# Cross entropy with label smoothing: first row in three tiles, second row in eleven of which nine follow into its buffers, first row's logarithm behind the second row's first exponential

## The chip, the cores and the metric

The kernel runs on one core of one Trainium2 chip. The metric is the device time in microseconds; times are medians. A *span* is the stretch from the first to the last traced instruction of one execution. It is shorter than the time.

## The reference

For each of 256 rows of 32000 float32 logits it computes the cross entropy against a smoothed one-hot target:

```python
log_probs = logits - max(logits); log_probs -= log(sum(exp(log_probs)))
target    = eps / C everywhere, plus (1 - eps) at the label
out       = -sum(target * log_probs)
```

Unfolded, a row's loss is `log(sum(exp(x))) - eps/C * sum(x) - (1 - eps) * x[label]`. The draw is from a normal distribution, and the kernel leaves the maximum out. Three things are needed of each row: the sum of exponentials, the sum of logits, and one gathered logit.

## The kernel before

Each of the 128 partitions holds two rows, streamed one after the other in tiles. For each tile ScalarE makes the exponentials (only their sum is kept, the elements go to a discard buffer) and VectorE the sum of logits. GpSimd gathers the labels' logits. At the end TensorE transposes the results into one row, for one contiguous output transfer; matmuls on a tile of row two warm its clock up for that.

```python
WIDTHS = ((8000, 8000, 8000, 8000),
          (8000, 6272, 4736, 3648, 2688, 2048, 1536, 1216, 1024, 832))
RING_MIN = 4736      # wider or equal: one of three ring buffers; narrower: its own buffer
TURN_MAX = 3648      # wider: single discard buffer; narrower or equal: one of three in turn
# ... cut ...
def sum_exps(xt, w, out):
    if w > TURN_MAX:
        ja = junk.tile([P, max(WIDTHS[0])], BF16, name="ja", tag="ja")   # bufs=1
    else:
        ja = turn.tile([P, TURN_MAX], BF16, name="jt", tag="jt")         # bufs=3
    nc.scalar.activation(out=ja[:, :w], in_=xt[:, :w], func=AF.Exp, accum_out=out)
# ... cut: the first row's loop, then its halves added up ...
nc.scalar.activation(out=lse[:], in_=sums[:, 1, :], func=AF.Ln)   # before row two
# ... cut: row two, where the last exponential's sum goes to PSUM ...
nc.scalar.activation(out=lse[:], in_=elast[:], func=AF.Ln, bias=done[2][:, 1:2])
```

The softmax here doesn't subtract the row's maximum and nothing guards it: scores larger than these inputs give would overflow.

## Time and profile before

| | before |
|---|---|
| time, 3 runs | 84.93 us (84.86 to 85.04) |
| span of the profiled run | 83.2 us |
| last tile's VectorE sum starts (my landing clock) | 79.13 us |
| last exponential | 79.24 to 80.12 us |
| last logarithm starts | 80.20 us |
| busy: DVE, ACT | 45%, 71% of the span |

The busy share of 71% for ScalarE is an average over a first row with idle stretches of some 2.5 us between tiles and a second row with almost none from its second tile on. So one reads the second row. These timeline lines of the kernel before (start, length, engine, line, operation, idle time and what ended it) show the two exponentials of row two that write to the single discard buffer after another that did, and the first that does not:

```profile
57.77 5.43 ACT L188 ACTIVATE ja<-xt 128x6272 bf16<-128x6272 f32 x1 [0.50 <-DMA xt<-in_logits_dram]
63.10 0.19 ACT L188 ACTIVATION_READ_ACCUMULATOR ja<-xt 128x1 f32 x1
63.41 4.15 ACT L188 ACTIVATE ja<-xt 128x4736 bf16<-128x4736 f32 x1
67.47 0.19 ACT L188 ACTIVATION_READ_ACCUMULATOR ja<-xt 128x1 f32 x1
67.72 3.24 ACT L188 ACTIVATE jt<-xl 128x3648 bf16<-128x3648 f32 x1
```

The 6272 exponential and its accumulator read are over at 63.10 + 0.19 = 63.29; the next starts at 63.41, together with VectorE's sum of the same tile (63.42). It waited for data. Whatever it also had to wait for on its own engine lay inside that wait.

### The profile page before, as it was taken

To read this page: it belongs to the slowest core of one execution; us is meant where nothing else is said; L and a number is where in the kernel's file an instruction comes from. 1 tells how busy PE (TensorE), PEld (TensorE's weight loads), DVE (VectorE), ACT (ScalarE), POOL (GpSimd) and SP (SyncE) were. 2 spreads that over 40 slices of the span, in tenths; PEclk is the share of its full clock that TensorE was granted. 3 is DMA by queue.
4 is the path that set the end of the run, shared out by engine and by line. 5 is a ranking of instruction groups with operands and counts; after the bars stand their busy time and mean duration, and the time that the engine had idled before them with its cause. 6 is when DMAs were issued, how large, how long until landed. Compare 5 with 4: busy or idle time off the path is not lost.

```text
span 83.2 us, 230 instructions
## 1 busy us (share of the span) xinstructions
PE 7.0 (8%) x23; PEld 5.0 (6%) x23; DVE 37.1 (45%) x35; ACT 58.8 (71%) x31; POOL 5.7 (7%) x19
## 2 busy tenths in 40 slices
PE   0000000000000000000000010000000000899020
PEld 0000000000000000000000000000000000787000
DVE  0000005950495009910397017922944736754860
ACT  5000005997499809994399908997999999999960
POOL 3201640031000000000000040000000000000000
PEclk9999999999999999999999999999999999999995
DMA  5999999997999899989998998998999999999600
GB/s 131 416 416 408 454 423 462 477 447 323 477 493 431 369 431 493 446 369 416 493 462 354 416 439 386 495 447 370 428 420 414 442 407 415 412 414 412 256 0 0
DMA packets 2258, 32.77 MB, mean 394 GB/s; under 512 B 337, under 2 KB 338, under 8 KB 850
## 3 DMA queue, kind: packets, MB, share of 16 engines
q1 hardware_dynamic: 2018, 30.72, 87.4%
q10 hardware_dynamic: 144, 2.05, 5.8%
q0 software_dynamic: 96, 0.00, 0.1%
HBM read 32.77 MB, written 0.00 MB: 394 GB/s over the span
## 4 chain that ended last, share of the span: by engine, by line
DMA 64%; ACT 32%; issue 1%; SPq 0%; PE 0%; DVE 0%; ACTq 0%
DMA xt<-in_logits_dram 40%; DMA xl<-in_logits_dram 23%; ACT ja L188 17%; ACT jt L188 15%; SPq L167 0%; PE lse_t L193 0%; DVE res L284 0%; ACT lse L279 0%; ACTq L188 0%
## 5 line engine op out<-in xcount | busy, mean ns | idle before, releaser
L188 ACT ACTIVATE ja<-xt 128x8000 bf16<-128x8000 f32 (+2 forms) x7 | 43.9, 6276 | 20.1 <-DMA xt<-in_logits_dram 20.0
L173 DVE SCALAR_TENSOR_TENSOR jd<-xt 128x4000 f32<-128x4000 f32 (+2 forms) x7 | 27.7, 3954 | 33.6 <-DMA xt<-in_logits_dram 33.6
L188 ACT ACTIVATE jt<-xl 128x3648 bf16<-128x3648 f32 (+6 forms) x7 | 12.2, 1748 | 0.1
L173 DVE SCALAR_TENSOR_TENSOR jd<-xl 128x1824 f32<-128x1824 f32 (+6 forms) x7 | 7.9, 1125 | 5.2 <-DMA xl<-in_logits_dram 5.0
L270 PE MATMUL warm<-xl,ident 128*128 128x256 f32 x20 | 6.1, 471 | 21.4 <-DMA xl<-in_logits_dram 21.4
L270 PEld LDWEIGHTS warm<-xl,ident 128*128 128x128 f32 x20 | 4.8, 246 | 22.5 <-DMA xl<-in_logits_dram 21.7
L193 PE MATMUL loss_t<-ident,loss 128*1 128x128 f32 x1 | 0.4, 372 | 49.2 <-POOL loss L224 49.2
L193 PEld LDWEIGHTS loss_t<-ident,loss 128*1 128x1 f32 x1 | 0.1, 79 | 49.2 <-POOL loss L224 49.2
L226 DVE COPY res<-loss_t 1x128 f32<-1x128 f32 x1 | 0.3, 278 | 4.5 <-PE loss_t L193 4.5
L211 POOL TENSOR_TENSOR half<-sums 128x4 f32<-128x4 f32 x1 | 0.2, 198 | 28.2 <-ACT ja L188 28.2
L125 POOL DMA_INDIRECT gat<-in_logits_dram,flat_idx x2 | 2.0, 1004 | 0.7 <-POOL ident masks.py:199 0.4
L92 ACT ACT_TABLE_LOAD x1 | 1.3, 1283 | 0.9 <-PEq L311 0.9
L188 ACT ACTIVATION_READ_ACCUMULATOR ja<-xt 128x1 f32 x7 | 1.3, 186 | 0.0
L188 ACT ACTIVATION_READ_ACCUMULATOR jt<-xl 128x1 f32 x7 | 1.3, 181 | 0.0
L146 POOL TENSOR_SCALAR weighted<-gat 128x1 f32<-128x1 f32 x1 | 0.8, 763 | 5.8 <-DMA gat<-in_logits_dram,flat_idx 5.8
L105 POOL DMA_DIRECT2D lab<-in_labels_dram x1 | 0.8, 766 | 1.0 <-POOLq L311 1.0
L216 ACT ACTIVATE lse<-half 128x1 f32<-128x1 f32 x1 | 0.2, 203 | 0.6 <-POOL half L211 0.6
L173 DVE DVE_READ_ACCUMULATOR jd<-xt 128x1 f32 x7 | 0.6, 82 | 0.0
L173 DVE DVE_READ_ACCUMULATOR jd<-xl 128x1 f32 x7 | 0.6, 82 | 0.0
L117 POOL TENSOR_TENSOR flat_idx<-rowoff,lab 128x2 int32<-128x2 int32 x1 | 0.2, 197 | 5.4 <-DMA lab<-in_labels_dram 5.4
L193 PE MATMUL lin_t<-ident,done 128*1 128x128 f32 x1 | 0.3, 270 | 3.0 <-DVE done L263 3.0
L282 DVE COPY lin_row<-lin_t 1x128 f32<-1x128 f32 x1 | 0.3, 278 | 0.4 <-PE lin_t L193 0.4
(20 smaller groups left out, 3.8 us busy)
## 6 DMA issues: line engine op xcount, KB each, us to landing
xt<-in_logits_dram SPq DMA_DIRECT2D x4, 4000.0 KB, 21.1
xt<-in_logits_dram SPq DMA_DIRECT2D x1, 3136.0 KB, 19.4
xt<-in_logits_dram SPq DMA_DIRECT2D x1, 2368.0 KB
xt<-in_logits_dram SPq DMA_DIRECT2D x1, 2000.0 KB, 11.5
xt<-in_logits_dram ACTq DMA_DIRECT2D x1, 2000.0 KB, 13.2
xl<-in_logits_dram SPq DMA_DIRECT2D x1, 1824.0 KB, 19.5
xl<-in_logits_dram SPq DMA_DIRECT2D x1, 1344.0 KB, 22.3
xl<-in_logits_dram SPq DMA_DIRECT2D x1, 1024.0 KB, 24.3
```

Of the source, the lines that this page charges most:

```text
L92: nc.scalar.add_instruction(mybir.InstLoadActFuncSet(name=nc.get_next_instruction_name(), act_func_set_id=tbl, ins=[], outs=[],))
L105: nc.gpsimd.dma_start(out=lab[:], in_=labels.bitcast(I32).rearrange("(p f) -> p f", p=P))
L117: nc.gpsimd.tensor_tensor(out=flat_idx[:], in0=rowoff[:], in1=lab[:].rearrange("p (r two) -> p r two", two=2)[:, :, 0:1], op=ALU.add,)
L125: nc.gpsimd.indirect_dma_start(out=gat[:, r : r + 1], out_offset=None, in_=logits[:], in_offset=bass.IndirectOffsetOnAxis(ap=flat_idx[:, r ...
L146: nc.gpsimd.tensor_scalar(out=weighted[r], in0=gat[:, r : r + 1], scalar1=label_weight, scalar2=None, op0=ALU.mult,)
L173: return nc.vector.scalar_tensor_tensor(out=jd[:, :h], in0=xt[:, :h], scalar=1.0, in1=xt[:, h:w], op0=ALU.mult, op1=ALU.add, accum_out=out,)
L188: nc.scalar.activation(out=ja[:, :w], in_=xt[:, :w], func=AF.Exp, accum_out=out)
L193: nc.tensor.transpose(out=row[:], in_=column, identity=ident[:])
L211: nc.gpsimd.tensor_tensor(out=half[:], in0=sums[:, :, :n], in1=sums[:, :, n:], op=ALU.add)
L226: nc.vector.tensor_copy(out=res[:, :, r : r + 1], in_=loss_t[:])
L270: nc.tensor.matmul(warm[:], lhsT=ident[:], rhs=xt[:, i * WARM_COLS : (i + 1) * WARM_COLS], start=True, stop=True,)
L282: nc.vector.tensor_copy(out=lin_row[:], in_=lin_t[:])
```

## The change

The intent: ask for all of row one without waiting for a buffer to come free, let row two follow into the same three buffers, end on a narrower tile (640 columns in place of 832), and keep the first row's logarithm from making ScalarE wait for GpSimd. The core of the diff, cut:

```diff
 WIDTHS = (
-    (8000, 8000, 8000, 8000),
-    (8000, 6272, 4736, 3648, 2688, 2048, 1536, 1216, 1024, 832),
+    (9600, 11200, 11200),
+    (8320, 6528, 4672, 3392, 2496, 1856, 1408, 1088, 896, 704, 640),
 )
-RING_MIN = 4736
-TURN_MAX = 3648
+FOLLOW = (1, 2, 6)      # how many tiles of row two go into each buffer of row one
+TURN_MAX = 2496
-WARM_LEFT, WARM_COLS = 5, 256
+WARM_LEFT, WARM_COLS = 6, 256
 ... (cut: the three wide buffers and their slices)
+        with tc.issue_after(exps.ins):
+            nc.scalar.activation(out=lse[:], in_=total[:, 1, :], func=AF.Ln)
 ... (cut: two additions in a row on GpSimd in place of a tree; the copy of row one's result, now behind row two's first sum)
+        if t == 0:
+            finish_first_row(part, exps)
```

More of the change, by code (lines that the diff above doesn't have):

```diff
@@ L78 @@
     c_big = 1.0 - eps
-    ring = ctx.enter_context(tc.tile_pool(name="ring", bufs=3))
+    wide = ctx.enter_context(tc.tile_pool(name="wide", bufs=1))
     tail = ctx.enter_context(tc.tile_pool(name="tail", bufs=1))
@@ L154, with load @@
     res = small.tile([1, P, R], FP32, name="res", tag="res")
-    def load(w: int, col: int, name: str):
-        if w >= RING_MIN:
-            xt = ring.tile([P, max(WIDTHS[0])], FP32, name="xt", tag="xt")
-        else:
-            xt = tail.tile([P, w], FP32, name=name, tag=name)
+    assert R == 2 and len(FOLLOW) == len(WIDTHS[0])
+    buffers = []
+    for r in range(R):
+        for b, w in enumerate(WIDTHS[0]):
+            widths = WIDTHS[0][b : b + 1]
+            if r == 1:
+                t = sum(FOLLOW[:b])
+                widths = WIDTHS[1][t : t + FOLLOW[b]]
+            buf = wide.tile([P, w], FP32, name=f"wide{b}_{r}", tag=f"wide{b}")
+            assert sum(widths) <= w
+            at = 0
+            for v in widths:
+                buffers.append(buf[:, at : at + v])
+                at += v
+    for t in range(sum(FOLLOW), len(WIDTHS[1])):
+        w = WIDTHS[1][t]
+        buffers.append(tail.tile([P, w], FP32, name=f"tail{t}", tag=f"tail{t}")[:])
+    def load(w: int, col: int):
+        xt = buffers.pop(0)
         if col == 0:
@@ L166, in load @@
         else:
-            nc.sync.dma_start(out=xt[:, :w], in_=x[:, col : col + w])
+            nc.sync.dma_start(out=xt, in_=x[:, col : col + w])
         return xt
@@ L181, in sum_logits, with sum_exps @@
         )
-    def sum_exps(xt, w: int, out: bass.AP) -> None:
+    def sum_exps(xt, w: int, out: bass.AP):
         if w > TURN_MAX:
@@ L187, in sum_exps @@
             ja = turn.tile([P, TURN_MAX], BF16, name="jt", tag="jt")
-        nc.scalar.activation(out=ja[:, :w], in_=xt[:, :w], func=AF.Exp, accum_out=out)
+        return nc.scalar.activation(
+            out=ja[:, :w], in_=xt[:, :w], func=AF.Exp, accum_out=out
+        )
     def row_of(column: bass.AP, name: str):
@@ L194, in row_of, with finish_first_row @@
         return row
+    assert R == 2
     col = 0
-    for r in range(R - 1):
-        n = len(WIDTHS[r])
-        sums = small.tile([P, 2, n], FP32, name=f"sums{r}", tag=f"sums{r}")
-        for t, w in enumerate(WIDTHS[r]):
-            xt = load(w, col, f"xl{r}_{t}")
-            col += w
-            sum_logits(xt, w, sums[:, 0, t : t + 1])
-            sum_exps(xt, w, sums[:, 1, t : t + 1])
-        while n > 1:
-            assert n % 2 == 0
-            n //= 2
-            half = small.tile([P, 2, n], FP32, name=f"half{r}_{n}", tag=f"half{r}_{n}")
+    n = len(WIDTHS[0])
+    sums = small.tile([P, 2, n], FP32, name="sums", tag="sums")
+    for t, w in enumerate(WIDTHS[0]):
+        xt = load(w, col)
+        col += w
+        sum_logits(xt, w, sums[:, 0, t : t + 1])
+        sum_exps(xt, w, sums[:, 1, t : t + 1])
+    def finish_first_row(part, exps) -> None:
+        total = sums[:, :, 0:1]
+        for t in range(1, n):
+            acc = small.tile([P, 2, 1], FP32, name=f"acc{t}", tag=f"acc{t}")
             nc.gpsimd.tensor_tensor(
-                out=half[:], in0=sums[:, :, :n], in1=sums[:, :, n:], op=ALU.add
+                out=acc[:], in0=total, in1=sums[:, :, t : t + 1], op=ALU.add
             )
-            sums = half
-        lse = small.tile([P, 1], FP32, name=f"lse{r}", tag=f"lse{r}")
-        nc.scalar.activation(out=lse[:], in_=sums[:, 1, :], func=AF.Ln)
-        lin = small.tile([P, 1], FP32, name=f"lin{r}", tag=f"lin{r}")
-        nc.gpsimd.tensor_tensor(out=lin[:], in0=sums[:, 0, :], in1=weighted[r], op=ALU.add)
-        scaled = small.tile([P, 1], FP32, name=f"scaled{r}", tag=f"scaled{r}")
+            total = acc[:]
+        lin = small.tile([P, 1], FP32, name="lin0", tag="lin0")
+        nc.gpsimd.tensor_tensor(
+            out=lin[:], in0=total[:, 0, :], in1=weighted[0], op=ALU.add
+        )
+        scaled = small.tile([P, 1], FP32, name="scaled0", tag="scaled0")
         nc.gpsimd.tensor_scalar(
@@ L222 @@
         )
-        loss = small.tile([P, 1], FP32, name=f"loss{r}", tag=f"loss{r}")
+        lse = small.tile([P, 1], FP32, name="lse0", tag="lse0")
+        with tc.issue_after(exps.ins):
+            nc.scalar.activation(out=lse[:], in_=total[:, 1, :], func=AF.Ln)
+        loss = small.tile([P, 1], FP32, name="loss0", tag="loss0")
         nc.gpsimd.tensor_tensor(out=loss[:], in0=scaled[:], in1=lse[:], op=ALU.add)
-        loss_t = row_of(loss[:], f"loss_t{r}")
-        nc.vector.tensor_copy(out=res[:, :, r : r + 1], in_=loss_t[:])
+        loss_t = row_of(loss[:], "loss_t0")
+        with tc.issue_after(part.ins):
+            nc.vector.tensor_copy(out=res[:, :, 0:1], in_=loss_t[:])
     r = R - 1
-    n = len(WIDTHS[r])
+    last = len(WIDTHS[r]) - 1
     elast = psum.tile([P, 1], FP32, name="elast", tag="elast")
@@ L240 @@
     for t, w in enumerate(WIDTHS[r]):
-        left = n - 1 - t
-        xt = load(w, col, f"xl{r}_{t}")
+        left = last - t
+        xt = load(w, col)
         col += w
@@ L247 @@
         if left == 0:
-            sum_exps(xt, w, elast[:])
+            exps = sum_exps(xt, w, elast[:])
         elif left <= 2:
-            sum_exps(xt, w, pairs[2 - left][:, 1:2])
+            exps = sum_exps(xt, w, pairs[2 - left][:, 1:2])
         else:
-            sum_exps(xt, w, esum[:, t : t + 1])
+            exps = sum_exps(xt, w, esum[:, t : t + 1])
+        if t == 0:
+            finish_first_row(part, exps)
         if left == 2:
```

## The prediction

> **What bounds the kernel now.** I read the chain that ended last first, then the slices of DMA activity, then the timeline of the second row tile by tile, and last the groups of instructions with the shapes kept apart.
>
> The chain and the DMA slices of the page of the kernel before:
>
> ```profile
> DMA  5999999997999899989998998998999999999600
> ...
> DMA 64%; ACT 32%; issue 1%; SPq 0%; PE 0%; DVE 0%; ACTq 0%
> ```
>
> Transfers are busy from the second slice to slice 38 of 40, so the stream of 32.77 MB hardly stops (a 7 or 8 is followed by fuller slices). The ACT share of the chain is not a second bound: the chain goes back through ScalarE in stretches in which a buffer's release by ScalarE started a later transfer, or in which ScalarE and the transfers kept step. Nor do the long waits of the DMA-issuing queue (24.7 us for VectorE, 10.4 us for ScalarE, 16.2 us for earlier transfers) cost stream time. The fourth wide tile is asked for when the first is read, at 20.35 us; the second has then not quite landed and the third is queued whole. Something was in the queue throughout.
>
> How fast is the stream? The VectorE sum of a tile is short and usually idle before the tile comes, so its start is my clock for the landing (some 0.1 us late). Timeline of the kernel before, columns start, length, engine, line, operation:
>
> ```profile
> 40.81 4.33 DVE L173 SCALAR_TENSOR_TENSOR jd<-xt 128x4000 f32<-128x4000 f32 x1 [5.14 <-DMA xt<-in_logits_dram]
> 50.32 4.33 DVE L173 SCALAR_TENSOR_TENSOR jd<-xt 128x4000 f32<-128x4000 f32 x1 [0.42 <-DMA xt<-in_logits_dram]
> 57.78 3.43 DVE L173 SCALAR_TENSOR_TENSOR jd<-xt 128x3136 f32<-128x3136 f32 x1 [3.13 <-DMA xt<-in_logits_dram]
> 63.42 2.62 DVE L173 SCALAR_TENSOR_TENSOR jd<-xt 128x2368 f32<-128x2368 f32 x1 [2.21 <-DMA xt<-in_logits_dram]
> ```
>
> 8000 columns take 50.32 - 40.81 = 9.51 us, 6272 take 7.46 and 4736 take 5.64. From the last two: 1.82/1536 = 1.185 ns a column; over all tiles down to the 1216-column one (76.91 us) 1.178 ns a column plus about 0.07 us a transfer fits best. 4.096 MB in 9.5 us is 431 GB/s.
>
> The end of the timeline of the kernel before:
>
> ```profile
> 76.90 1.22 ACT L188 ACTIVATE jt<-xl 128x1216 bf16<-128x1216 f32 x1
> 76.91 0.79 DVE L173 SCALAR_TENSOR_TENSOR jd<-xl 128x608 f32<-128x608 f32 x1 [0.55 <-DMA xl<-in_logits_dram]
> ...
> 78.12 0.69 DVE L173 SCALAR_TENSOR_TENSOR jd<-xl 128x512 f32<-128x512 f32 x1
> 78.18 1.06 ACT L188 ACTIVATE jt<-xl 128x1024 bf16<-128x1024 f32 x1
> ...
> 79.13 0.59 DVE L173 SCALAR_TENSOR_TENSOR jd<-xl 128x416 f32<-128x416 f32 x1
> 79.14 0.19 ACT L188 ACTIVATION_READ_ACCUMULATOR jt<-xl 128x1 f32 x1
> 79.24 0.88 ACT L188 ACTIVATE jt<-xl 128x832 bf16<-128x832 f32 x1
> ...
> 80.20 0.26 ACT L279 ACTIVATE lse<-elast,done 128x1 f32<-128x1 f32 x1
> ```
>
> The exponential of each tile starts together with its VectorE sum (76.90 and 76.91): it too starts at the landing, with ScalarE barely free. Only the last is late: its data are there at 79.13, ScalarE starts at 79.24, because the one before (78.18 + 1.06) ends there. So the kernel is bound by the stream until about 79.1 us, and then by one small exponential of 0.88 us and about 3 us of final work. All that a better order can win is in that exponential and the 0.1 us before it.
>
> **What the Trainium skill says.** The page "DMA: Bandwidth & Descriptors", section "Where 436 GB/s comes from", gives 435.2 GB/s as the ceiling of the 16 ports; the 431 GB/s above agree, so larger transfers have no rate to win. The same page, section "Issuing engines are not separate DMA queues", says that transfers run on the same 16 engines whoever issued them; issuing earlier is then worth nothing while the queue is not empty. The page "ScalarE: Activation LUTs", section "What ACT_TABLE_LOAD costs", gives 186 ns + 0.833 ns a column for an activation, with back-to-back activations overlapping by about 93 ns. The trace agrees on the slope:
>
> ```profile
> L188 ACT ACTIVATE ja<-xt 128x8000 bf16<-128x8000 f32 x5 | 34.4, 6870 | 19.5 <-DMA xt<-in_logits_dram 19.5
> L188 ACT ACTIVATE jt<-xl 128x1024 bf16<-128x1024 f32 x1 | 1.1, 1057 | 0.0
> ```
>
> (6870 - 1057)/6976 = 0.8333 ns a column, fixed part 1057 - 853 = 204 ns. The last one, which writes to PSUM, has 880 - 693 = 187 ns. The overlap is seen too: the accumulator read starts at 79.14 and takes 0.19 us, the next exponential starts at 79.24.
>
> **The change part by part.**
>
> 1. Row one in three transfers. The first tile is still two halves on two queues; four transfers instead of five in the row, eleven instead of ten in the second: 15 and 15, the same bytes. The stream ends where it did, at about 79.13 to 79.2 us on the landing clock. Row one on ScalarE: the third tile lands at 40.81 - 0.07 = 40.74, and its 11200 columns take 0.204 + 9.333 = 9.54 us, until 50.28. The first tile of row two lands at 40.74 + 8320 x 0.001178 + 0.07 = 50.61. Still in time, 0.3 us of slack.
>
> 2. Buffers. All of row one can be asked for at once; 8320 waits for the read of the first tile (about 24 us), the next two for that of the second (27.5 + 9.5 = 37 us), six more for that of the third (50.3 us), and then at some 0.45 us apiece. At 50.3 us 6528 and 4672 are still queued, to 63.9 us. The stream is not starved, but it was not before either: worth 0.
>
> 3. The logarithm of row one. Before: 0.20 us at 48.35, in a gap of ScalarE that ended at 50.31. After: behind the 8320 exponential, which ends at 50.61 + 7.14 = 57.75, to about 58.0; the 6528 columns come at 50.61 + 7.69 + 0.07 = 58.37. Hidden in both: 0. VectorE's copy of row one's result now stands ahead of the 6528 sum, may hold it back by half a microsecond, and VectorE recovers it before the next tile.
>
> 4. The eleven widths. Landings from 58.37 on, each by width x 1.178 ns + 0.07: 4672 at 63.94, 3392 at 68.01, 2496 at 71.02, 1856 at 73.28, 1408 at 75.01, 1088 at 76.36, 896 at 77.49, 704 at 78.39, 640 at 79.21. ScalarE from 58.37, by 0.204 + width x 0.8333 ns: 6528 takes 5.64. The next two, 4672 and 3392, are wider than 2496 and so write to the single discard buffer again, and an exponential into it has to wait until the one before is wholly finished. Estimate from the trace: the accumulator read starts 0.09 before the end and takes 0.19, and the last logarithm started 0.03 after such a read, so 0.13 us each instead of none. In the kernel before this wait lay beside waits for data; here ScalarE has no data to wait for. So 4672 starts at 58.37 + 5.64 + 0.13 = 64.14, 3392 at 64.14 + 4.10 + 0.13 = 68.37, 2496 at 68.37 + 3.03 = 71.40, then back to back 1856 at 73.68, 1408 at 75.43, 1088 at 76.81, 896 at 77.92, 704 at 78.87, 640 at 79.66, until 79.66 + 0.72 = 80.38. Each starts 0.1 to 0.5 us after its landing: ScalarE, not the stream, sets the end.
>
> Sum: 80.38 against 79.24 + 0.88 = 80.12 before is +0.26 us. The last tile is 0.16 us shorter (720 against 880 ns), but it starts 0.42 us later. The final work is unchanged. 84.93 + 0.26 = 85.19; since a step error of 0.02 us over ten steps is as likely to the good side, I put it at 85.15.
>
> **The rivals.**
>
> Stream-bound to the end: if the discard buffer costs nothing and ScalarE's steps are a trifle shorter, the 640 exponential starts at its landing, about 79.2, and ends at 79.92, 0.2 us before the old end: 84.7 us. For it: the widths look made for that. Against: even without the 0.13 us twice, the same sum ends at 80.12, a draw.
>
> False sharing: if reading one slice of a refilled buffer waited for all transfers into it, the six slices in the third buffer would wait for 896 at 77.49 us, with 11136 columns of exponentials (10.5 us) and two more tiles still to do: 77.5 + 10.5 + 1.5 = 89.5 against 80.1, about 94 us. Against it: in the trace VectorE's 512-wide sum starts at 78.12 while ScalarE's accumulator read into the other column of the same small tile runs from 78.02 to 78.21, so accesses seem to be kept apart by region.
>
> A cold final transpose: the row-one transpose took 372 ns, the final two 270 ns each, thanks to the warming matmuls. The new tile gives 9 rather than 10 of them (18 records, not 20), so they end some 0.4 us earlier, and the end comes later. The page "TensorE: Matmul & The Clock Gate", section on the HAM clock gate, gives a free-running window of 3413 ns; in the trace the granted clock drops at about 80.8 us, just after the last transpose. If it dropped earlier, +0.1 us. I count 0.02.
>
> **Range and chances.** The floor is the stream, 84.7; the sum is 85.15; doubled discard waits or a cold transpose make 85.5. A range of 84.8 to 85.5 allows for the run-to-run spread of 0.18 us. Over 2% faster would need the stream to end 1.7 us sooner, at over 440 GB/s: 0.01. Over 2% slower needs false sharing or a starved stream: 0.03. Within 2%: 0.96.
>
> **What would show it.** Right: in the second row each exponential from 4672 on starts 0.1 to 0.5 us after its VectorE sum and directly after the one before, with no wait for a transfer; 4672 and 3392 start about 0.13 us after the end of their predecessors; the last exponential ends near 80.4; the logarithm lies between 57.7 and 58.1. Wrong: a wait of ScalarE for a transfer in the last nine tiles, a last landing off 79.2 by over 0.2 us, a DMA slice below 7 between 42 and 77 us, or wide gaps between exponentials of one refilled buffer.

## The result, and the profile after

| | before | after |
|---|---|---|
| time, 6 runs each | 84.88 us (84.82 to 85.04) | 85.06 us (85.02 to 85.25) |
| ratio | | 1.0022, 95% interval 1.0009 to 1.0035 |
| spans of the runs | 83.2 us, profiled | 83.2, 83.2, 83.2, 83.3, 83.3, 83.5 us |

A ratio is the mean time of one kernel's runs over that of the other's of the same rounds, so it is not quite the ratio of the medians. The change costs about 0.2 us: small, within 2%, and clear of the noise. The prediction was 85.15 with a range of 84.8 to 85.5.

Two profiles of the changed kernel exist, both of runs at the slow end (85.25 and 85.21 us). The DMA slices and the chain of the first, to be laid beside those of before:

```profile
DMA  6999999999799879977997999999999999999600
...
DMA 57%; ACT 36%; issue 2%; PE 0%; DVE 0%; ACTq 0%
DMA wide<-in_logits_dram 57%; ACT ja L204 27%; ACT jt L204 9%; PE lse_t L211 0%; DVE res L310 0%; ACT lse L305 0%; ACTq L204 0%
```

The stream fills the same 38 slices as before (the page of the kernel before is quoted in the prediction). The chain has moved from transfers (64% to 57%) to ScalarE (32% to 36%). The place where it moved is the second row. Timeline of the second profile of the changed kernel:

```profile
58.37 5.64 ACT L204 ACTIVATE ja<-wide 128x6528 bf16<-128x6528 f32 x1 [0.43 <-DMA wide<-in_logits_dram]
...
63.95 2.59 DVE L189 SCALAR_TENSOR_TENSOR jd<-wide 128x2336 f32<-128x2336 f32 x1 [1.46 <-DMA wide<-in_logits_dram]
64.14 4.10 ACT L204 ACTIVATE ja<-wide 128x4672 bf16<-128x4672 f32 x1
...
68.02 1.93 DVE L189 SCALAR_TENSOR_TENSOR jd<-wide 128x1696 f32<-128x1696 f32 x1 [1.47 <-DMA wide<-in_logits_dram]
68.36 3.03 ACT L204 ACTIVATE ja<-wide 128x3392 bf16<-128x3392 f32 x1
...
71.03 1.46 DVE L189 SCALAR_TENSOR_TENSOR jd<-wide 128x1248 f32<-128x1248 f32 x1 [1.07 <-DMA wide<-in_logits_dram]
71.39 2.27 ACT L204 ACTIVATE jt<-wide 128x2496 bf16<-128x2496 f32 x1
73.29 1.13 DVE L189 SCALAR_TENSOR_TENSOR jd<-wide 128x928 f32<-128x928 f32 x1 [0.79 <-DMA wide<-in_logits_dram]
73.66 1.74 ACT L204 ACTIVATE jt<-wide 128x1856 bf16<-128x1856 f32 x1
...
79.13 0.49 DVE L189 SCALAR_TENSOR_TENSOR jd<-tail 128x320 f32<-128x320 f32 x1
79.55 0.72 ACT L204 ACTIVATE jt<-tail 128x640 bf16<-128x640 f32 x1
...
80.35 0.26 ACT L305 ACTIVATE lse<-elast,done 128x1 f32<-128x1 f32 x1
80.67 0.08 PEld L211 LDWEIGHTS lse_t<-ident,lse 128*1 128x1 f32 x1 [0.63 <-ACT lse L305]
80.67 0.37 PE L211 MATMUL lse_t<-ident,lse 128*1 128x128 f32 x1 [0.44 <-ACT lse L305]
```

Read the DVE and ACT lines in pairs. VectorE's sum marks the landing; before, the exponential started with it. Now 4672 starts 0.19 us behind its data and 3392 0.34 us behind. The two steps are 64.14 - 58.37 = 5.77, 0.13 more than the 5.64 us of the exponential itself, and 68.36 - 64.14 = 4.22, 0.12 more than 4.10. From 2496 on the exponentials stand back to back (71.39 + 2.27 = 73.66) and keep the lag: the last data are there at 79.13, as before, but the last exponential starts at 79.55 and ends at 80.27, 0.15 us later than before. VectorE is itself busy until just before the last tile, so there its start could mislead; the completion events of the last transfer, which the packed traces keep, say 79.11 us in both.

These two profiled runs each have something more that the median does not. In the first, the whole stream lands 0.14 to 0.16 us later, in row one already (VectorE starts on the third tile at 40.91 us there, and at 40.75 in the profile of e1_no_discard_wait below); its last exponential ends at 80.42, so 0.15 us late again once the stream's 0.14 to 0.16 are taken off. In the second, the last transpose took 0.37 us, as the last line shows, where before it took 0.27.

### The profile page after: what moved, and what is told of

Same layout as the page of the kernel before. It is cut to its first block, busy times and chain, and to the rows that moved or that the text cites. A ratio compares the mean times of both kernels' runs of the same rounds, so it can differ in the third digit from the quotient of the medians.

```text
span 83.5 us, 226 instructions
## 1 busy us (share of the span) xinstructions
PE 7.4 (9%) x21; PEld 5.2 (6%) x21; DVE 36.9 (44%) x35; ACT 58.3 (70%) x31; POOL 12.6 (15%) x19
## 4 chain that ended last, share of the span: by engine, by line
DMA 57%; ACT 36%; issue 2%; PE 0%; DVE 0%; ACTq 0%
DMA wide<-in_logits_dram 57%; ACT ja L204 27%; ACT jt L204 9%; PE lse_t L211 0%; DVE res L310 0%; ACT lse L305 0%; ACTq L204 0%
## 5 line engine op out<-in xcount | busy, mean ns | idle before, releaser
L204 ACT ACTIVATE ja<-wide 128x11200 bf16<-128x11200 f32 (+5 forms) x7 | 47.2, 6741 | 21.5 <-DMA wide<-in_logits_dram 21.5
L189 DVE SCALAR_TENSOR_TENSOR jd<-wide 128x5600 f32<-128x5600 f32 (+10 forms) x12 | 34.5, 2876 | 39.9 <-DMA wide<-in_logits_dram 39.9
L296 PE MATMUL warm<-wide,ident 128*128 128x256 f32 x18 | 6.5, 537 | 12.3 <-DMA wide<-in_logits_dram 12.3
L204 ACT ACTIVATE jt<-wide 128x2496 bf16<-128x2496 f32 (+4 forms) x5 | 7.4, 1478 | 0.0
L296 PEld LDWEIGHTS warm<-wide,ident 128*128 128x128 f32 x18 | 5.0, 284 | 13.6 <-DMA wide<-in_logits_dram 12.6
L236 POOL TENSOR_TENSOR lin<-acc,weighted 128x1 f32<-128x1 f32 x1 | 4.4, 4382 | 0.1
L147 POOL TENSOR_SCALAR weighted<-gat 128x1 f32<-128x1 f32 x1 | 3.4, 3411 | 5.4 <-DMA gat<-in_logits_dram,flat_idx 5.4
L204 ACT ACTIVATE jt<-tail 128x704 bf16<-128x704 f32 (+1 forms) x2 | 1.5, 746 | 0.0
L204 ACT ACTIVATION_READ_ACCUMULATOR ja<-wide 128x1 f32 x7 | 1.3, 187 | 0.0
L189 DVE SCALAR_TENSOR_TENSOR jd<-tail 128x352 f32<-128x352 f32 (+1 forms) x2 | 1.0, 508 | 0.0
```

Source lines behind the costliest of these rows:

```text
L147: nc.gpsimd.tensor_scalar(out=weighted[r], in0=gat[:, r : r + 1], scalar1=label_weight, scalar2=None, op0=ALU.mult,)
L189: return nc.vector.scalar_tensor_tensor(out=jd[:, :h], in0=xt[:, :h], scalar=1.0, in1=xt[:, h:w], op0=ALU.mult, op1=ALU.add, accum_out=out,)
L204: return nc.scalar.activation(out=ja[:, :w], in_=xt[:, :w], func=AF.Exp, accum_out=out)
L236: nc.gpsimd.tensor_tensor(out=lin[:], in0=total[:, 0, :], in1=weighted[0], op=ALU.add)
L296: nc.tensor.matmul(warm[:], lhsT=ident[:], rhs=xt[:, i * WARM_COLS : (i + 1) * WARM_COLS], start=True, stop=True,)
```

## The experiments

**The theories.** A: the loss is the two waits of about 0.13 us for the single discard buffer, on a ScalarE chain that has no slack from the second tile of row two on; the narrower last tile gives back a part. B: the larger transfers of row one make the stream land later, as the first profile seems to show. Further parts to be cleared: the logarithm's move, and the first row and the buffers by themselves. The runs of a group share a chip and the runs of the kernel before.

| run | time us | ratio to before (95% interval) | mean span (before) | time less span |
|---|---|---|---|---|
| e1_no_discard_wait | 84.78 | 0.9990 (0.9971 to 1.0008) | 82.95 (83.06) | 1.82 |
| e5_all_discard_waits | 86.03 | 1.0139 (1.0115 to 1.0163) | 84.25 (83.06) | 1.79 |
| e2_row2_widths_of_before | 85.14 | 1.0041 (1.0020 to 1.0062) | 83.12 (83.06) | 2.07 |
| e3_row2_widths_of_after | 85.56 | 1.0092 (1.0063 to 1.0120) | 83.67 (83.06) | 2.03 |
| e6_shift_128 | 84.74 | 0.9979 (0.9960 to 0.9999) | 82.95 (83.15) | 1.80 |
| e4_log_before_row2 | 85.15 | 1.0024 (1.0004 to 1.0044) | 83.37 (83.15) | 1.79 |
| e2d_one_more_transfer | 85.11 | 1.0018 (0.9999 to 1.0037) | 83.10 (83.15) | 2.04 |
| e3d_one_transfer_less | 85.70 | 1.0078 (1.0054 to 1.0103) | 83.60 (83.15) | 2.09 |
| e2p3_three_fillers | 84.98 | 1.0006 (0.9986 to 1.0025) | 83.18 (83.11) | 1.80 |
| e2p2_two_fillers | 85.34 | 1.0051 (1.0032 to 1.0070) | 83.13 (83.11) | 2.21 |
| after_again | 85.07 | 1.0019 (1.0000 to 1.0038) | 83.28 (83.11) | 1.80 |

The median of before was 84.84 us in the first group of four, 84.92 in the second and 84.83 in the last three. Its own time less span is 1.78 to 1.80. The time in the second column is the median; the last column is the mean time less the mean span, so it is not the difference of the columns shown. Mean spans are of values rounded to 0.1 us. All eleven gave correct results.

### The two waits taken away: e1_no_discard_wait

```diff
-TURN_MAX = 2496
+TURN_MAX = 4672
-    turn = ctx.enter_context(tc.tile_pool(name="turn", bufs=3))
+    turn = ctx.enter_context(tc.tile_pool(name="turn", bufs=2))
```

> The changed kernel, but the 4672 and 3392 exponentials write to a rotating discard buffer (two of 4672 columns) and so need not wait for the end of their predecessors. Theory A (the two waits of 0.13 us on ScalarE's full chain are the loss): both gaps go, the last exponential ends 0.26 us sooner than in the changed kernel, now almost at the landing of its data; time about 84.75 to 84.85, that is 0.1 to 0.15 us under the kernel before. Theory B (the first row's larger transfers make the stream land 0.14 us later, as the one profile shows: last tile at 79.27 instead of 79.13): the last tile still lands near 79.25 and the time stays within 0.1 us of the changed kernel, about 85.0.

Measured: 84.78 us. Against the changed kernel that is 0.9990/1.0022 = 0.9968, or 0.27 us less. The two ratios are from different chips, and their intervals alone would allow 0.1 to 0.5 us; the timeline is sharper:

```profile
58.36 5.65 ACT L204 ACTIVATE ja<-wide 128x6528 bf16<-128x6528 f32 x1 [0.43 <-DMA wide<-in_logits_dram]
64.01 4.08 ACT L204 ACTIVATE jt<-wide 128x4672 bf16<-128x4672 f32 x1
68.09 3.01 ACT L204 ACTIVATE jt<-wide 128x3392 bf16<-128x3392 f32 x1
71.10 2.27 ACT L204 ACTIVATE jt<-wide 128x2496 bf16<-128x2496 f32 x1
...
79.11 0.49 DVE L189 SCALAR_TENSOR_TENSOR jd<-tail 128x320 f32<-128x320 f32 x1
79.27 0.72 ACT L204 ACTIVATE jt<-tail 128x640 bf16<-128x640 f32 x1
```

Each exponential starts when the one before ends (58.36 + 5.65 = 64.01, and so on). From nearly the same start (58.36 against 58.37) the last one comes 0.28 us sooner, 79.27 against 79.55. It ends at 79.27 + 0.72 = 79.99, 0.13 us before the old end of 80.12: that is what the new widths give, and 0.28 less 0.13 is the 0.15 us that the change loses.

The last landing is at 79.11, with the same row one, so the late stream of the first profile is not a fixed cost of that row. It does come back in the profiled runs of e2d, e2p3 and e4 below (last tile at 79.25 to 79.30), all at or near the slow end of their runs. The kernel before was profiled once, but its spans too reach 83.5 us. That the new row one makes such runs no more frequent is shown only by the mean of e2p3 below. Against the kernel before, e1 is 0.06 us faster by the medians: not distinguishable, and less than the 0.1 to 0.15 expected.

### Seven more such waits: e5_all_discard_waits

```diff
-TURN_MAX = 2496
+TURN_MAX = 0
 ... (cut: a buffer's width, in a branch that is no longer reached)
```

> The changed kernel with every exponential writing to the single discard buffer: seven further waits, from 2496 to 640. Theory A: each of them costs about 0.12 to 0.13 us on a ScalarE that has no slack, so the last exponential ends 0.85 to 0.95 us later than in the changed kernel; time about 85.95. Theory B: ScalarE has room between landings, so most of them hide; time under 85.3.

Measured: 86.03 us; 1.0139/1.0022 = 1.0117, or 0.99 us over the changed kernel. Its timeline around two of the added waits:

```profile
71.38 2.28 ACT L204 ACTIVATE ja<-wide 128x2496 bf16<-128x2496 f32 x1
73.57 0.19 ACT L204 ACTIVATION_READ_ACCUMULATOR ja<-wide 128x1 f32 x1
73.79 1.75 ACT L204 ACTIVATE ja<-wide 128x1856 bf16<-128x1856 f32 x1
75.44 0.19 ACT L204 ACTIVATION_READ_ACCUMULATOR ja<-wide 128x1 f32 x1
75.66 1.38 ACT L204 ACTIVATE ja<-wide 128x1408 bf16<-128x1408 f32 x1
```

The next exponential starts 0.03 us after the end of the accumulator read (73.57 + 0.19 = 73.76, then 73.79), as the prediction's estimate had it. Without the wait it starts about 0.09 us after the *start* of that read. So the wait is worth 0.13 us, and a record after it is 0.015 us longer (1750 against 1735 ns for 1856 columns). Seven times 0.14 is 0.98 us: from the 6528 exponential to the end of the last one it is 22.89 us here and 21.90 in the second profile of the changed kernel. Nothing of it hides, and the measured 0.99 is a little over the 0.85 to 0.95 expected because of the longer records.

### Row one, buffers and logarithm alone: e2_row2_widths_of_before, then three more runs

```diff
-    (8320, 6528, 4672, 3392, 2496, 1856, 1408, 1088, 896, 704, 640),
+    (8000, 6272, 4736, 3648, 2688, 2048, 1536, 1216, 1024, 832),
-FOLLOW = (1, 2, 6)
+FOLLOW = (1, 2, 5)
-TURN_MAX = 2496
+TURN_MAX = 3648
-WARM_LEFT, WARM_COLS = 6, 256
+WARM_LEFT, WARM_COLS = 5, 256
```

> First row, buffers and logarithm as changed; the second row's ten widths, its discard limit of 3648 columns and its warming tile as in the kernel before. Theory A (loss lies in the second row's widths and discard limit alone): equal to the kernel before, 84.85 to 84.95, with ScalarE starting each tile at its landing. Theory B (the stream lands later because of the first row): 85.0 to 85.05, every landing 0.14 us later than before.

Measured: 85.14 us, more than either theory expected (B had 85.0 to 85.05). The landings were not late (last one at 79.04) and the spans equal those of before, 83.12 against 83.06. The excess lies outside the span: 2.07 us between time and span instead of 1.78. A first guess was the number of loads, 14 here, which changes the semaphore of the output transfer:

```diff
+    spare = small.tile([1, 4], I32, name="spare", tag="spare")
+    nc.sync.dma_start(out=spare[:], in_=labels.bitcast(I32)[0:4].rearrange("(p f) -> p f", p=1))
```

> The run with the second row's old widths was equal to the kernel before inside the traced span (83.0 to 83.3 against 82.9 to 83.4 us), but its time was 2.05 us above the span, not 1.77, and its output transfer was awaited second to last at the end, not last. Here one transfer of 16 bytes that nobody uses is added, so that there are again 15 loads and the output transfer takes the same semaphore as in the kernel before. If the excess belongs to that count and not to the first row's transfers: 84.85 to 84.95. If it belongs to the first row or the buffers: 85.1 again.

Measured: 85.11 us, and still 2.04 us outside the span, with the output transfer awaited last again. The guess was wrong. What did go with the excess was the number of VectorE instructions in the trace (semaphore instructions included, which the page's counts leave out). It was 57 in the kernels before and after, e1, e4, e5 and e6, all at 1.78 to 1.82 us, and 54, 54, 59 and 60 in the other four. So fillers were added to the e2 kernel, at the start, where VectorE has nothing to do:

```diff
+    for i in range(3):                      # 2 in the second run
+        nop = small.tile([P, 1], FP32, name=f"nop{i}", tag=f"nop{i}")
+        nc.vector.memset(nop[:], 0.0)
```

> The run with the second row's old widths (first row, buffers and logarithm as changed), with three one-element-wide VectorE memsets added at the start, where VectorE is idle for 15 us. So far the six kernels with 57 VectorE instructions in the trace have 1.75 to 1.85 us between time and span, those with 54, 59 and 60 have 2.0 to 2.2. With three fillers there are 57 again. If the excess goes with VectorE's instruction count: time less span about 1.8, time 84.85 to 84.95, equal to the kernel before, as theory A has it for the first row, the buffers and the logarithm. If it belongs to the first row or the buffers: 85.1 again.

> The same with two memsets, 56 VectorE instructions. If the excess goes with an exact number of instructions: still 2.05 us above the span, time 85.1. If only a smaller count is at fault: 84.9.

Measured: with three fillers 1.80 us outside the span and a ratio of 1.0006; with two fillers 2.21 us and 1.0051, at nearly equal spans (83.18 and 83.13); 2.21 is more than the 2.05 expected. The excess comes and goes with memsets that do no work for the result. Whether it is their number, or the place to which they move the instructions behind them, these runs don't tell apart, and why it happens is open. With it gone, the first row in three tiles, the buffers and the moved logarithm together are within the noise of the kernel before, as the prediction's parts 1 to 3 had it; of the three only the logarithm is tried alone (e4 below), so parts that cancel are not excluded. The changed kernel beside them:

> The changed kernel itself beside them on the same chip: theory A expects 0.15 to 0.25 us over the kernel before, in time and in span alike, and over the run with three fillers as well; chance (a good or bad chip) would show as a difference within 0.05.

Measured: 85.07 us, ratio 1.0019, span 0.17 us over that of before: the first result again, though with this interval (1.0000 to 1.0038) only just outside the noise.

### The second row's widths alone: e3_row2_widths_of_after, e3d_one_transfer_less

The edit on the kernel *before*, cut (the ring and discard buffers follow the widest tile, and the warming tile is that of the changed kernel), and what the second run adds:

```diff
-    (8000, 6272, 4736, 3648, 2688, 2048, 1536, 1216, 1024, 832),
+    (8320, 6528, 4672, 3392, 2496, 1856, 1408, 1088, 896, 704, 640),
-RING_MIN = 4736
+RING_MIN = 4672
-TURN_MAX = 3648
+TURN_MAX = 2496
# e3d only:
-            nc.sync.dma_start(out=xt[:, :h], in_=x[:, :h])
-            nc.scalar.dma_start(out=xt[:, h:w], in_=x[:, h:w])
+            nc.sync.dma_start(out=xt[:, :w], in_=x[:, :w])
 ... (cut: only this one transfer, no second one from ScalarE's queue, is issued ahead of the rest)
```

> The kernel before (first row in four, ring of three buffers, logarithm where it was), with only the second row's eleven widths, the discard limit of 2496 columns and the warming tile of the changed kernel. One transfer more than the changed kernel, 16 instead of 15, so its landings are 0.07 us later. Theory A: the whole loss is here: the same two waits of 0.13 us, time 85.05 to 85.2. Theory B: no loss beyond the extra transfer: 84.85 to 84.95.

> The kernel before with the second row's widths of the changed kernel, now with the first tile loaded by one transfer in place of two halves, so 15 loads again. The run with 16 loads had 2.05 us outside its span too, and awaited the output transfer before five other semaphores at the end (0.25 us). Theory A (second row's widths and the two discard waits): the same end as the changed kernel, 85.0 to 85.15. If the first row or the buffers matter: 85.3 and more, or 84.9 and less.

Measured: 85.56 and 85.70 us, some 0.4 and 0.55 us over what theory A allowed at most: a miss. These kernels have 60 and 59 VectorE instructions and 2.03 and 2.09 us outside the span, which takes off 0.25 to 0.3. The rest is in the span, 0.61 and 0.45 us over before. The two waits are there (timeline of e3):

```profile
58.73 5.64 ACT L188 ACTIVATE ja<-xt 128x6528 bf16<-128x6528 f32 x1 [0.52 <-DMA xt<-in_logits_dram]
...
64.50 4.10 ACT L188 ACTIVATE ja<-xt 128x4672 bf16<-128x4672 f32 x1
...
68.72 3.03 ACT L188 ACTIVATE ja<-xl 128x3392 bf16<-128x3392 f32 x1
```

64.50 - 58.73 - 5.64 = 0.13 and 68.72 - 64.50 - 4.10 = 0.12 us. But the stream of both profiled runs was late, the last tile at 79.47 in e3 and 79.69 in e3d, 0.34 and 0.56 us behind before, of which, in e3, one transfer more explains 0.07. Both profiled runs are at the slow end (86.05 and 86.08 us, where the fastest of the six took 85.43 and 85.39), so they show a bad run rather than a typical one. In e3 the slowest of the 16 parts of a transfer landed 0.39 us behind all others in the first tile, and 0.38 to 0.44 us behind in every later one. In e3 the output transfer is also awaited second of six at the end, which lengthens the time from its issue to the end of the span from 2.02 to 2.25 us. What makes the stream late in these two kernels is open; they show the two waits, but they do not measure the widths' cost.

### The logarithm back ahead of row two: e4_log_before_row2

```diff
-        with tc.issue_after(exps.ins):
-            nc.scalar.activation(out=lse[:], in_=total[:, 1, :], func=AF.Ln)
+        nc.scalar.activation(out=lse[:], in_=total[:, 1, :], func=AF.Ln)
 ... (cut: the copy likewise, and finish_first_row called before row two's loop)
```

> The changed kernel with the first row's logarithm and result copy issued ahead of the second row's first exponential, as in the kernel before. ScalarE waits for GpSimd's two additions and then starts the 8320 exponential about 0.4 us later (near 51.1 us), which ends near 58.3, still at or before the landing of 6528 (58.4). If the move is worth nothing (my reading): within 0.1 us of the changed kernel, 85.0 to 85.15. If the move is what protects the chain: 0.3 to 0.4 us slower, 85.4 or more.

Measured: 85.15 us, ratio 1.0024 against the changed kernel's 1.0022 and 1.0019. Timeline of e4:

```profile
50.87 0.20 ACT L244 ACTIVATE lse<-acc 128x1 f32<-128x1 f32 x1 [0.36 <-POOL acc L231]
...
50.98 7.12 ACT L204 ACTIVATE ja<-wide 128x8320 bf16<-128x8320 f32 x1
...
58.50 5.64 ACT L204 ACTIVATE ja<-wide 128x6528 bf16<-128x6528 f32 x1 [0.31 <-DMA wide<-in_logits_dram]
```

ScalarE does wait 0.36 us for GpSimd, but it still waits another 0.31 us for the 6528 columns afterwards. The move buys slack in a place that had slack.

### A version that takes what the widths can give: e6_shift_128

```diff
 (on top of e1_no_discard_wait)
-    (8320, 6528, 4672, 3392, 2496, 1856, 1408, 1088, 896, 704, 640),
+    (8448, 6400, 4672, 3392, 2496, 1856, 1408, 1088, 896, 704, 640),
```

> The kernel of the run without the two discard waits, with 128 columns moved from the second to the first tile of row two (8448 and 6400 for 8320 and 6528). There ScalarE still ran some 0.1 to 0.16 us behind the landings from 4672 on. Theory A: the second tile lands as before but its exponential is 0.107 us shorter, so the whole chain behind it comes 0.05 to 0.1 us sooner, until the landings bind; time 0.05 to 0.1 us under that run, 84.7, and 0.15 to 0.2 us under the kernel before on the same chip. If the stream already bound the end there, nothing changes.

Measured: 84.74 us, ratio 0.9979 to before, an interval that just leaves 1 out. Timeline of e6:

```profile
70.94 2.28 ACT L204 ACTIVATE jt<-wide 128x2496 bf16<-128x2496 f32 x1
70.95 1.46 DVE L189 SCALAR_TENSOR_TENSOR jd<-wide 128x1248 f32<-128x1248 f32 x1 [1.08 <-DMA wide<-in_logits_dram]
...
79.05 0.49 DVE L189 SCALAR_TENSOR_TENSOR jd<-tail 128x320 f32<-128x320 f32 x1
...
79.14 0.72 ACT L204 ACTIVATE jt<-tail 128x640 bf16<-128x640 f32 x1
```

Exponential and sum start together again, and the last tile waits 0.09 us where the changed kernel's waits 0.42. That beats both kernels, by about 0.2 us against before. For this last tile the stream now binds nearly to the end: by its completion event it landed at 79.03, its exponential starts 0.11 us later, and the 896 exponential, which did wait for its data, starts 0.09 us after its own landing (77.33, then 77.42). Whether other widths would give more was not tried.

## Why the prediction was right

**The stream ends where it did (part 1): right.** The last landing was predicted at 79.13 to 79.2 us on the landing clock and is at 79.13 in the second profile (part 4 had 79.21). In the first it was 79.27, but with every tile of that run late.

**The buffers are worth nothing (part 2): not contradicted.** e2 with three fillers, 1.0006, but with row one and the logarithm changed along.

**The logarithm is hidden in both places (part 3): right**, from e4. In the first profile VectorE's sum of the 6528 tile starts at 59.09, 0.56 us after the exponential, and the next sum is on time.

**The two discard waits (part 4): right, in place and in size.** Predicted 0.13 us each at 4672 and 3392; measured 0.13 and 0.12. Taking them away gives back 0.27 us, seven more cost 0.99.

**The sum: 0.26 us predicted for the last exponential's end, 0.15 measured, about 0.2 in the time.** The term that was off is the fixed part of an exponential that starts without any wait. The prediction took 204 ns from records that had all waited, and put the 187 ns of the last one down to its sum going to PSUM. That reading was wrong: that exponential was the one that had not waited. In e5, where the last one waits and its sum goes to PSUM just the same, it takes 736 - 533 = 203 ns; in the six back-to-back ones into SBUF, from 2496 to 704, the fixed part is about 187 ns (1735 - 1547 for 1856 columns, 1095 - 907 for 1088). Six such steps at 0.017 us are 0.10 us. The prediction had named an error of 0.02 us a step and put 0.04 us off for it. So the mechanism was right, but that 85.15 came within 0.1 us of 85.06 is in part luck: the interval of the ratio, 0.08 to 0.30 us, holds both 0.15 and 0.26 and can't tell them apart. What lies between 0.15 us and the 0.2 of the time may be runs like the second profile, where the last transpose was slower by 0.10 us; two profiles don't show it.

**The rivals.** Stream-bound to the end is what e6 is, at 84.74 us where the rival had 84.7; it needed the discard waits gone and 128 columns moved. The draw that the prediction saw without the waits was 0.13 us too pessimistic (e1 ends at 79.99, not 80.12), by the same 0.10 us of fixed parts for the most part. False sharing: no sign, the six slices of the third buffer are read one by one as they land. The cold transpose was given 0.02 us. It happens: in the profile of after_again the granted clock drops at about 80.35 us, ahead of the transpose, in those of before, e1 and e6 behind it. In e5 it drops at 81.48, just ahead of a transpose at 81.53 that takes 0.37 us too.

## What to carry to other kernels

When tile widths are tuned so that an engine is free just as each tile lands, the schedule has no room for fixed costs of a tenth of a microsecond. Find out which of the engine's instructions share a buffer that only it writes: here each such pair on a full chain cost 0.14 us, and the wait that cost nothing beside a wait for data was paid in full once the data were early. And read spans beside times when a control run surprises: the difference between the two changed here by 0.4 us (2.21 to 1.80) when two idle instructions became three.

## What the Trainium skill lacked or had wrong

- "ScalarE: Activation LUTs", section "What ACT_TABLE_LOAD costs": its 186 ns + 0.833 ns a column hold for back-to-back exponentials (1735 ns for 1856 columns, which is 188 ns fixed), and its overlap of about 93 ns is seen between an exponential and the accumulator read behind it (in e5, 73.57 against an end at 73.66). The page does not say that an exponential which waited, for a transfer or for its own engine, took some 16 ns more in nearly every case here (1750 ns), nor what one pays that has to wait for the completion of its predecessor: 0.13 us, beside the 16 ns.
- No page that I read has it: the time outside the traced span was 1.78 to 1.82 us in the kernels with 57 VectorE instructions, 2.04 to 2.07 with 54, 2.21 with 56 and 2.03 to 2.09 with 59 and 60. Those with 54, 56 and one of those with 57 (e2 and its variants) do the same work.
- No page that I read says whether a part of the stream that falls behind catches up. In e3 it did not: the slowest of the 16 parts of a transfer was 0.39 us behind the next in the first tile, 0.41 in the third and 0.38 in the last. In the kernel before a gap of 0.10 us in the first tile was 0.01 in the second, so this is no rule.
- "TensorE: Matmul & The Clock Gate", section "Part 1: The HAM clock gate": the free-running window of 3413 ns fits; the stretch of full granted clock after the warming matmuls was 6.83 us, two windows, in most profiles and 3.41 us in that of after_again. That the same kernel's last transpose therefore takes 270 ns in one run and 373 ns in another is worth a line there: the page says of the start of the fast stretch that it varies from run to run, not of its end.
- "SBUF — State Buffer", section "Who interferes with whom", lacks nothing here: VectorE and GpSimd share a port pair that is an exclusive lock for a whole instruction, also where the VectorE instruction has two SBUF inputs and the GpSimd one reads SBUF. The trace agrees: in the first profile of the changed kernel a one-column addition on GpSimd took 4.38 us, where before it took 0.19; it started at 50.93, beside a VectorE sum that started at 50.77 and took 4.49 us, and it ended with that sum. In e4, where that sum comes later, the same addition took 0.19 us. It cost nothing here, since the logarithm starts only at 57.90.
